# Second mixer: three blocks of the first token tile at its start, and two transposes queued later

## The chip, the cores and the metric

One core of one Trainium2 chip runs the whole program in one launch. The metric is device microseconds from launch to end; the number used is the median of several runs. Engines in the profile: PE is TensorE (PEld its weight loads), DVE is VectorE, ACT is ScalarE, POOL is GpSimd, SP is SyncE, which issues the transfers.

## The reference, cut to what matters

The program computes two blocks, each of two layers, on 256 tokens of width 1024, in float32. The first block has, per layer, a feed-forward part, a mixer and a second feed-forward part. The second block has, per layer, one mixer and one feed-forward part. The change touches only the mixer of the second block, so it acts twice in a run:

```python
h = rms_norm(x, norm_mix_g) * (1 + sc_m) + sh_m
proj = h @ w_in                                   # (256, 1024) @ (1024, 5024)
(qa, ka, va, cq, ckv, kr, qc, kc, vc, ga, gb, gc) = jnp.split(proj, idx, axis=-1)
o_na  = neighborhood_attention(qa, ka, va, na_rpb)            # 4 heads of 64
q_b   = rms_norm(cq, mla_q_norm_g) @ mla_w_uq                 # cq: 256 columns
kv_b  = rms_norm(ckv, mla_kv_norm_g) @ mla_w_ukv              # ckv: 128 columns
k_pe  = rope_2(kr, pos_t)                                     # kr: 32 columns
o_mla = blocked_attention(q_full, k_full, v_b, ...)           # 4 heads of 96
q_c   = axial_rope(rms_norm(qc), pos_row, pos_col)            # 8 heads of 64
k_c   = axial_rope(rms_norm(kc), pos_row, pos_col)            # 2 heads of 64
o_gqa = blocked_attention(q_c, k_c, v_c, ...)
merged = sigmoid(ga) * (o_na @ w_br_na) + sigmoid(gb) * (o_mla @ w_br_mla) + sigmoid(gc) * (o_gqa @ w_br_gqa)
x = x + g_m * (merged @ w_out)
```

## The kernel before

**Precision and weights.** Every big product is made of three matmuls on pairs (high part, rest), so each weight unit (128 rows by up to 1024 numbers) is loaded by a transfer, cast on ACT to its high part (`prep_H`, line 321) and subtracted on DVE for the rest (`prep_L`, through the helper of line 185). A block of 512 columns of `w_in` is four units, each of two row steps (kt); one unit of 832 columns belongs to the odd block of 416 columns.

**The planner's clock.** While the program is written out, `pump` advances a clock of its own: 0.648 for a row step of a 512-column block, 0.528 for one of the 416-column block, 0.327 for one of `gemmA`. On each pump one more unit is prepared if `hold` is off, fewer than `WH` units are live, and 1.2 have gone by since the last one. `hold` is set when the last results of a stage are merged, and `fin_b` for the second tile clears it. Work given to `later` or `spawn` is written out when that clock reaches its due time. Afterwards a list scheduler orders each engine's instructions by its own estimate of what is ready; on the chip each engine works through its list in that order.

**Tokens.** There are two token tiles of 128. The input of the mixer for tile 1 is finished late: `fin_a` makes the normalised tile (line 198), and `pend()`, which is `fin_b` for tile 1, transposes it on PE (line 182), scales it on DVE and ACT (lines 200 and 206) and splits it into `uH` (line 214) and `uL`.

**The opening of the mixer (`mix2`).** Block b0 holds the 512 columns of qc, block b1 va and cq, block b2 (the odd one, 416 columns) ckv, kr, kc and vc, and one more block holds qa and ka. The order of PE's work is: b0 for tile 0, half of b1 for tile 0, `pend()`, the other half, b0 for tile 1, b1 for tile 1, then `gemmA` for qa and ka (both tiles at once, in two halves). Then two lanes of neighbourhood attention start, and beside them come b2 for tile 0 and tile 1, then the gates. The products go to two PSUM banks of tag A in turn, so a block can start only when the copy of the block before the last has left its bank: line 1454 for q of tile 0, line 1464 for q of tile 1, line 1442 for b1, line 1493 for b2.

**After a block.** `q_post` squares q on ACT, sums on DVE (line 1408), takes the root on POOL (lines 219 and 221), and 3.45 of the planner's clock later multiplies, rotates (`rope`, line 185) and, another 5.6 later, transposes the heads on PE (four transposes from `m` to `T`) and copies them out (line 1426). The same chain runs for the keys in b2. `low_rank` normalises cq or ckv and transposes it 4.5 later (`gain_T`).

**Buffers.** SBUF tiles of 4 KB per partition share one pool of 36 (`m4`, tag s4): units, loads on their way, and the copies of q1, of b1 and of b2 among them. Tiles of 2 KB share a pool of 15 (`m2`). At the start of the mixer eight units are prepared, those of b0 and b1; `WH` is 8.

Of the kernel before, what the change touches and what calls it, by code (L numbers as in the profile page):

```python
# [103 lines left out]
class K:  # L104
# [1254 lines left out]
    def mix2_plan(self, l):  # L1359
        a = self.a  # L1360
        w = a["w_in_2_blk"][l]
        for i in (2, 1, 0):
            self.plan_cols(w[i])
        self.plan_cols(a["w_in_2_odd"][l])
        gate = lambda i: self.plan_cols(w[3 + i])
        gate(0)
        self.unit(2, a["mla_w_uq_2"][l])
        self.unit(1, a["mla_w_ukv_2"][l])
        gate(1), gate(4)
        self.plan_rows(a["w_br_na_2"][l], 0, 2)  # L1370
        gate(5), gate(2)
        self.plan_rows(a["w_br_gqa_2"][l], 0, 4)
        gate(3)
        self.plan_rows(a["w_br_mla_2"][l], 0, 2)
        self.plan_rows(a["w_out_2"][l], 0, 8)

    def mix2(self, l, u, pend):
# [24 lines left out]

        def gqa_norm(ps, nh, tab, tt, fin, pair=False):
            n = nh * 64
# [6 lines left out]
            def rest():  # L1411
                qn = self.m2([128, 512])
                self.mul(v(qn[:, :n], nh), v(ps, nh), r[:, :nh].unsqueeze(2).to_broadcast([128, nh, 64]))
                o = self.m2([128, 512])
                self.rope(o, qn, nh, 64, tab[:, 0, tt], tab[:, 1, tt], 2, pair)
                yield 5.6
                fin(o)
# [3 lines left out]
        def q_post(tt, ps):  # L1421
# [5 lines left out]

            gqa_norm(ps[:, :], 8, gt[0], tt, fin, True)

        def low_rank(ps, n, H, L, g):  # L1430

            sq = self.m2([128, 512])
            ss = self.sm([128, 1])
            self.act(sq[:, :n], ps, AF.Square, accum_out=ss)
            r = self.rstd(ss, 1, n)
            c = self.m2([128, 256])
            self.ts(c[:, :n], ps, r, ALU.mult)
            self.later(4.5, lambda: self.gain_T(c, H, L, g, n // 128))

# [9 lines left out]

        b0, b1 = self.blk(), self.blk()  # L1450
        p = self.pA()
# [3 lines left out]
        p = self.pA()  # L1455
        self.gemmB(u, b1, 0, p, k1=4)
        pend()
        q_post(0, q0)
        self.gemmB(u, b1, 0, p, k0=4)
        vc_post(0, p)  # L1460
        p = self.pA()
        self.gemmB(u, b0, 1, p, last=True)
# [4 lines left out]
        self.gemmB(u, b1, 1, p, last=True)  # L1467
        vc_post(1, p)

        qaT, kaT = self.m2([128, 2, 256]), self.m2([128, 2, 256])  # L1470
# [13 lines left out]
        lanes = [self.spawn(na[0:1], 0.95), self.spawn(na[1:2], 3.5)]  # L1484

        kvH, kvL = self.m2([128, 2, 128], F32R), self.m2([128, 2, 128], F32R)
        kpe = self.t([128, 2, 32], "kpe", 1)
        b = self.blk()
        for tt in range(2):
            p = self.pA()  # L1490
            self.gemmB(u, b, tt, p, 416, last=tt == 1)
            kv = self.m4([128, 512])
            nc.scalar.copy(kv[:, :416], p[:, :416])
            p = kv
            low_rank(p[:, 0:128], 128, kvH[:, tt:tt + 1], kvL[:, tt:tt + 1], self.vec("mkn", l, 1))
            self.rope(kpe[:, tt], p[:, 128:160], 1, 32, self.cs("mlac", tt * 32, 32), self.cs("mlas", tt * 32, 32), 1)
            nc.scalar.copy(vd[:, tt], p[:, 288:416])

            def fin(o, tt=tt):
                q = self.pT()  # L1500
                self.tr(q[:, 0:128], o[:, 0:128])
                nc.scalar.copy(kgT[:, tt * 128:tt * 128 + 128], q[:, 0:128])

            gqa_norm(p[:, 160:288], 2, gt[1], tt, fin)

# [382 lines left out]
```

## Time and profile before

| | |
|---|---|
| median of 3 runs | 1924.72 us (1924.52 to 1927.49) |
| the profiled execution, its own time | 1923.49 us |
| its span, first to last instruction | 1921.7 us |
| PE, PEld, DVE, ACT, POOL busy | 98%, 81%, 76%, 51%, 3% |
| granted TensorE clock, mean | 0.996 |
| opening of the second mixer, layer 0 | about 1134 to 1190 us of the span |
| opening of the second mixer, layer 1 | about 1526 to 1580 us of the span |

The busy share of PE says how little is left in all. What a change in one stage is worth is read from that stage: the stretches in which PE stands still, what it waited for, and how long its matmuls take just afterwards. All times below are microseconds from the start of the span. In a timeline row the bracket at the end gives how long the engine was idle before the row, and which instruction ended that idle time.

### The profile page before, as it was taken

The page shows a single profiled execution, that of the slowest core. Times are in us where ns is not written, and L with a number is a line of the kernel's source. Part 1 is how long each engine was busy: PE and PEld are TensorE (multiplying, and loading weights), DVE is VectorE, ACT ScalarE, POOL GpSimd, SP SyncE. Part 2 cuts the span into 40 slices and gives each one's busy share as a digit, 9 for nine tenths or more (in the row PEclk, how much of TensorE's full clock was granted, in tenths as well). Part 3 has the DMA queues.
Part 4 walks back from the last instruction along what each step waited for, and adds up shares of the span by engine and source line. Part 5 has one row for each costly group of instructions (what it writes and reads, how often), then busy time and mean ns, then how long its engine had stood idle before and what let it go on. Part 6 is the DMA issues. An engine that isn't in the chain of part 4 may idle for free.

```text
span 1921.7 us, 25594 instructions
## 1 busy us (share of the span) xinstructions
PE 1884.8 (98%) x9240; PEld 1554.0 (81%) x9240; DVE 1455.0 (76%) x2254; ACT 988.6 (51%) x1649; POOL 66.5 (3%) x135
## 2 busy tenths in 40 slices
PE   8999999999999999999999989999999999999998
PEld 6888798888888888988888878777888887778886
DVE  8877788787878877696878767678878776787552
ACT  6544566554445444476644445744544457546441
POOL 0000000100000000000100021000000110000000
PEclk9999999999999999999999999999999999999999
DMA  9997685488877987764498856468888763676540
GB/s 393 343 339 282 227 299 197 134 293 311 314 262 275 315 322 250 267 215 143 174 322 307 299 152 178 141 235 291 297 313 313 203 184 123 217 273 228 192 161 22
DMA packets 139056, 471.17 MB, mean 245 GB/s; under 512 B 24273, under 2 KB 24497, under 8 KB 138802
## 3 DMA queue, kind: packets, MB, share of 16 engines
q1 hardware_dynamic: 138930, 469.55, 70.3%
q8 instruction: 72, 1.18, 0.2%
q14 instruction: 54, 0.44, 0.1%
HBM read 468.40 MB, written 1.10 MB: 244 GB/s over the span
## 4 chain that ended last, share of the span: by engine, by line
PE 65%; issue 27%; DVE 4%; ACT 1%; POOL 1%; DMA 1%; SPq 0%; DVEq 0%; POOLq 0%; ACTq 0%
PE A L170 42%; PE B L170 19%; PE T L182 3%; DVE s L185 2%; DVE m L185 1%; DMA s<-in_ada_w 1%; PE T L170 1%; ACT m L206 0%; ACT s L321 0%; DVE s L515 0%; POOL sm L229 0%; POOL sm L221 0%; DVE h L185 0%; DVE m L203 0%; DVE s L203 0%
## 5 line engine op out<-in xcount | busy, mean ns | idle before, releaser
L170 PE MATMUL A<-s,uH 128*128 128x512 f32 (+1 forms) x2976 | 933.3, 394 | 2.1 <-ACT uH L214 1.4
L185 DVE TENSOR_TENSOR s<-s,s 128x1024 fp32r<-128x1024 f32 (+2 forms) x638 | 753.4, 1198 | 110.1 <-ACT s L321 104.0
L321 ACT CAST s<-s 128x1024 fp32r<-128x1024 f32 (+1 forms) x618 | 621.9, 1043 | 47.9 <-DVE s L185 28.7
L170 PEld LDWEIGHTS A<-s,uH 128*128 128x128 f32 x2976 | 548.0, 188 | 119.2 <-issue 7.3
L170 PE MATMUL A<-s,uL 128*128 128x512 f32 (+1 forms) x1488 | 579.9, 391 | 1.5 <-DVE uL L185 1.5
L170 PE MATMUL B<-s,m 128*128 128x512 f32 (+2 forms) x1696 | 407.4, 387 | 1.2 <-ACT m L214 1.1
L170 PEld LDWEIGHTS B<-s,m 128*128 128x128 f32 x1696 | 309.7, 189 | 62.8 <-ACT m L214 2.9
L170 PEld LDWEIGHTS A<-s,uL 128*128 128x128 f32 x1488 | 279.5, 188 | 61.1 <-DVE uL L185 4.0
L515 DVE SCALAR_TENSOR_TENSOR s<-s,cb 128x1024 f32<-128x1024 f32 x256 | 310.6, 1217 | 4.0 <-DMA s<-in_ada_w 3.4
L206 ACT ACTIVATE m<-A 128x256 f32<-128x256 f32 x126 | 48.3, 383 | 287.1 <-PE A L170 286.9
L214 ACT CAST m<-T 128x256 fp32r<-128x256 f32 x132 | 48.8, 372 | 205.7 <-PE T L182 205.7
L185 DVE TENSOR_TENSOR m<-m,A 128x256 f32<-128x256 f32 x126 | 52.6, 418 | 112.4 <-ACT m L206 111.8
L170 PE MATMUL A<-uH,s 128*128 128x256 f32 (+1 forms) x672 | 129.6, 289 | 2.7 <-ACT s L1442 2.3
L170 PEld LDWEIGHTS A<-uH,s 128*128 128x128 f32 (+1 forms) x672 | 107.0, 191 | 4.5 <-ACT s L1442 2.8
L170 PE MATMUL B<-s,s 128*128 128x512 f32 (+3 forms) x432 | 103.1, 383 | 2.5 <-DVE s L203 2.0
L170 PE MATMUL A<-uL,s 128*128 128x256 f32 (+1 forms) x336 | 96.3, 286 | 0.0
L185 DVE TENSOR_TENSOR m<-T,m 128x256 fp32r<-128x256 f32 x132 | 55.1, 420 | 54.2 <-ACT m L214 54.0
L170 PEld LDWEIGHTS B<-s,s 128*128 128x128 f32 (+1 forms) x432 | 78.6, 188 | 18.3 <-DVE s L203 2.9
L182 PE MATMUL T<-ident,m 128*128 128x128 f32 (+1 forms) x488 | 84.3, 273 | 8.1 <-DVE m L185 6.6
L182 PEld LDWEIGHTS T<-ident,m 128*128 128x128 f32 (+1 forms) x488 | 62.9, 139 | 35.2 <-DVE m L185 9.1
L206 ACT ACTIVATE m<-h 128x512 f32<-128x512 f32 x44 | 27.8, 632 | 84.3 <-DVE h L185 84.3
L170 PEld LDWEIGHTS A<-uL,s 128*128 128x128 f32 (+1 forms) x336 | 64.1, 191 | 0.7
(190 smaller groups left out, 1197.9 us busy)
## 6 DMA issues: line engine op xcount, KB each, us to landing
s<-in_ffn_gu SPq DMA_DIRECT2D x264, 512.0 KB, 5.2
s<-in_ada_w SPq DMA_DIRECT2D x240, 512.0 KB, 5.8
s<-in_w_in_blk SPq DMA_DIRECT2D x152, 512.0 KB, 4.8
s<-in_ffn_wd SPq DMA_DIRECT2D x88, 512.0 KB, 5.5
s<-in_ffn_w_down SPq DMA_DIRECT2D x44, 512.0 KB, 4.7
s<-in_w_out SPq DMA_DIRECT2D x40, 512.0 KB, 4.2
s<-in_final_ada_w SPq DMA_DIRECT2D x16, 512.0 KB, 6.5
s<-row SPq DMA_DIRECT2D x12, 512.0 KB, 6.5
```

The source lines that it names most:

```text
L170: self.last = self.nc.tensor.matmul(out, l, r, start=start, stop=stop, skip_group_check=True)
L182: self.nc.tensor.transpose(out, in_, self.ident[:p, :p])
L185: self.nc.vector.tensor_tensor(o, x, y, op=op)
L206: return self.nc.scalar.activation(o, x, f, **kw)
L214: self.nc.scalar.copy(H, x)
L321: self.last_H = self.nc.scalar.copy(H[:, :n], raw[:, :n])
L515: self.nc.vector.scalar_tensor_tensor(raw, raw, 1.0, self.cb, op0=ALU.mult, op1=ALU.mult, accum_out=v)
```

## The change

It moves b2 from after `gemmA` to the opening: b2 for tile 0 follows b1 for tile 0, b2 for tile 1 follows b1 for tile 1. The units of the odd block are therefore planned before those of qa and ka. `WH` is 12 during the opening and 8 after it. `hold` is cleared after the first half of b1, and `pend()` and `q_post` for tile 0 come after the whole of b1. The head transposes of q are due 9.0 instead of 5.6 after the rotation, those of the keys 7.0 instead of 5.6, and the transposes of `low_rank` 6.5 instead of 4.5.

```diff
 def mix2_plan(self, l):
-        for i in (2, 1, 0):
+        for i in (2, 1):
             self.plan_cols(w[i])
         self.plan_cols(a["w_in_2_odd"][l])
+        self.plan_cols(w[0])
...
-        def gqa_norm(ps, nh, tab, tt, fin, pair=False):
+        def gqa_norm(ps, nh, tab, tt, fin, wait, pair=False):
...
-                yield 5.6
+                yield wait
                 fin(o)
...
-            gqa_norm(ps[:, :], 8, gt[0], tt, fin, True)
+            gqa_norm(ps[:, :], 8, gt[0], tt, fin, 9.0, True)
...
-            self.later(4.5, lambda: self.gain_T(c, H, L, g, n // 128))
+            self.later(6.5, lambda: self.gain_T(c, H, L, g, n // 128))
...
-        b0, b1 = self.blk(), self.blk()
+        kvH, kvL = self.m2([128, 2, 128], F32R), self.m2([128, 2, 128], F32R)
+        kpe = self.t([128, 2, 32], "kpe", 1)
+
+        def odd_post(tt, p):
+            kv = self.m4([128, 512])
+            nc.scalar.copy(kv[:, :416], p[:, :416])
+            low_rank(kv[:, 0:128], 128, kvH[:, tt:tt + 1], kvL[:, tt:tt + 1], self.vec("mkn", l, 1))
+            self.rope(kpe[:, tt], kv[:, 128:160], 1, 32, self.cs("mlac", tt * 32, 32), self.cs("mlas", tt * 32, 32), 1)
+            nc.scalar.copy(vd[:, tt], kv[:, 288:416])
+
+            def fin(o):
+                q = self.pT()
+                self.tr(q[:, 0:128], o[:, 0:128])
+                nc.scalar.copy(kgT[:, tt * 128:tt * 128 + 128], q[:, 0:128])
+
+            gqa_norm(kv[:, 160:288], 2, gt[1], tt, fin, 7.0)
+
+        self.WH = 12
+        b0, b1, b2 = self.blk(), self.blk(), self.blk()
         p = self.pA()
         self.gemmB(u, b0, 0, p)
         q0 = self.m2([128, 512])
         nc.scalar.copy(q0, p)
         p = self.pA()
         self.gemmB(u, b1, 0, p, k1=4)
+        self.hold = False
+        self.gemmB(u, b1, 0, p, k0=4)
         pend()
         q_post(0, q0)
-        self.gemmB(u, b1, 0, p, k0=4)
         vc_post(0, p)
+        p = self.pA()
+        self.gemmB(u, b2, 0, p, 416)
+        odd_post(0, p)
         p = self.pA()
         self.gemmB(u, b0, 1, p, last=True)
...
         self.gemmB(u, b1, 1, p, last=True)
         vc_post(1, p)
+        p = self.pA()
+        self.gemmB(u, b2, 1, p, 416, last=True)
+        odd_post(1, p)
+        self.WH = 8
...
         lanes = [self.spawn(na[0:1], 0.95), self.spawn(na[1:2], 3.5)]
-
-        kvH, kvL = self.m2([128, 2, 128], F32R), self.m2([128, 2, 128], F32R)
-        kpe = self.t([128, 2, 32], "kpe", 1)
-        b = self.blk()
-        for tt in range(2):
-            p = self.pA()
-            self.gemmB(u, b, tt, p, 416, last=tt == 1)
...
```

The lines removed at the end did for b2 what `odd_post` now does.

## Rows read from the trace of the kernel before

**Rows 1.** The page's first part: busy time, share of the span and instructions of each engine.

```profile
PE 1884.8 (98%) x9240; PEld 1554.0 (81%) x9240; DVE 1455.0 (76%) x2254; ACT 988.6 (51%) x1649; POOL 66.5 (3%) x135
```

**Rows 2.** Stretches: window, length, busy PE, PEld, DVE, ACT, POOL; clock, DMA, GB/s.

```profile
1145.00:1150.00 5.00, 2.27 (x13) 1.61 (x13) 3.90 (x9) 2.19 (x6) 1.51 (x4) 1.00 0.60 156
...
1170.00:1175.00 5.00, 3.84 (x21) 3.60 (x20) 3.03 (x5) 4.15 (x8) 1.05 (x2) 0.66 0.64 168
```

**Rows 3.** Timeline of PE, opening of layer 0: start, length, instruction, [idle before].

```profile
1146.29 1.09 PE L182 MATMUL T<-ident,s 128*128 128x128 f32 x8 [1.39 <-DVE s L198]
...
1149.52 0.73 PE L170 MATMUL A<-s,uH 128*128 128x512 f32 x2 [1.45 <-ACT uH L214]
...
1150.58 0.62 PE L170 MATMUL A<-s,uH 128*128 128x512 f32 x2
...
1157.93 0.66 PE L182 MATMUL T<-ident,m 128*128 128x128 f32 x4 [0.57 <-DVE m L185]
...
1169.60 0.66 PE L182 MATMUL T<-ident,m 128*128 128x128 f32 x4 [1.40 <-DVE m L185]
1171.42 0.58 PE L170 MATMUL A<-uH,s 128*128 128x256 f32 x1 [1.16 <-ACT s L1442]
...
1174.58 0.41 PE L170 MATMUL A<-uH,s 128*128 128x256 f32 x2
...
1174.94 0.40 PE L170 MATMUL A<-uH,s 128*128 128x256 f32 x2
```

**Rows 4.** Timeline of PE, opening of layer 1.

```profile
1534.87 1.03 PE L182 MATMUL T<-ident,s 128*128 128x128 f32 x8
...
1546.76 0.66 PE L182 MATMUL T<-ident,m 128*128 128x128 f32 x4 [0.79 <-DVE m L185]
...
1551.15 0.28 PE L170 MATMUL A<-uH,s 128*128 128x256 f32 x1
...
1558.43 0.66 PE L182 MATMUL T<-ident,m 128*128 128x128 f32 x4 [1.36 <-DVE m L185]
1560.24 0.57 PE L170 MATMUL A<-uH,s 128*128 128x256 f32 x1 [1.16 <-ACT s L1442]
...
1563.89 0.40 PE L170 MATMUL A<-uH,s 128*128 128x256 f32 x2
```

**Rows 5.** Timeline of DVE, opening of layer 0.

```profile
1145.74 0.88 DVE L198 TENSOR_SCALAR s<-h,sm 128x512 f32<-128x512 f32 x2 [2.69 <-POOL sm L229]
...
1150.86 0.69 DVE L185 TENSOR_TENSOR uL<-m,uH 128x512 fp32r<-128x512 f32 x1 [0.67 <-ACT uH L214]
```

**Rows 6.** The chain of waits, layer 1: start, length, what.

```profile
1548.36 2.68 DVE s L185 x3
```

**Rows 7.** Timeline of ACT, opening of layer 1.

```profile
1545.16 0.59 ACT L1464 COPY s<-A 128x512 f32<-128x512 f32 x1
...
1559.12 0.58 ACT L1426 COPY s<-T 128x512 f32<-128x512 f32 x1 [8.72 <-PE T L182]
1559.60 0.59 ACT L1442 COPY s<-A 128x512 f32<-128x512 f32 x1
```

**Rows 8.** Groups by form, 1500 to 1600: xcount, busy us, mean ns.

```profile
L185 DVE TENSOR_TENSOR s<-s,s 128x832 fp32r<-128x832 f32 x4 | 4.1, 1018 | 0.0
```

**Rows 9.** Timeline of PE, layer 0: b2, the last attention output, the branches.

```profile
1182.42 0.53 PE L170 MATMUL A<-s,uH 128*128 128x416 f32 x2
...
1182.98 0.54 PE L170 MATMUL A<-s,uH 128*128 128x416 f32 x2
...
1282.28 1.08 PE L170 MATMUL B<-m,m 128*64 128x256 f32 x8
...
1284.09 11.05 PE L170 MATMUL A<-s,s 128*128 128x512 f32 x48
...
1300.42 2.88 PE L170 MATMUL A<-s,m 128*128 128x512 f32 x12
```

**Rows 10.** Waits of the transfer queue, 1120 to 1200: total us, times, longest.

```profile
SPq L306 <- PE A L170: 28.1, 11, 8.7
```

More of the change, by code (lines that the diff above doesn't have):

```diff
@@ L1484, in mix2 @@
         lanes = [self.spawn(na[0:1], 0.95), self.spawn(na[1:2], 3.5)]
-        kvH, kvL = self.m2([128, 2, 128], F32R), self.m2([128, 2, 128], F32R)
-        kpe = self.t([128, 2, 32], "kpe", 1)
-        b = self.blk()
-        for tt in range(2):
-            p = self.pA()
-            self.gemmB(u, b, tt, p, 416, last=tt == 1)
[L1492 to L1504, printed above, removed]
         gq = []
```

## The prediction

> **What bounds the kernel now.** The page's first part comes first: PE is busy 98% of the span [rows 1], so a change of order can win only what PE loses by standing still or by running slow. Next, the table by stretches over both openings of the second mixer: the reader is to see PE busy for 2.27 of 5 us in one stretch, and in another 3.84 of 5 at a granted clock of 0.66 [rows 2]. Then the timeline of PE, for what ended each pause.
>
> Layer 0 has five pauses in the opening [rows 3]. 1.39 us before the transposes of tile 1's input, which wait for the normalised tile. 1.45 us for `uH`, made from those transposes, because only one row step of b1 was left to run meanwhile. 0.57 and 1.40 us before the head transposes of q for tile 0 and tile 1, which wait for the end of the rotation on DVE. 1.16 us before the second half of `gemmA`, whose bank is still held: the copy of b1's tile 1 (line 1442) stands on ACT right behind the copy of those transposes. Sum 5.97.
>
> Layer 1 [rows 4] has its input transposes without a pause, then 0.79, 1.36 and the same 1.16. Sum 3.31.
>
> After the long pauses PE runs slow. From 1171.42 to 1174.58 five steps of `gemmA` take 3.16 us; the step from 1174.58 to 1174.94 takes 0.36, so 1.36 us are lost [rows 3], in a stretch that was partly at the 1.2 GHz level. In layer 1 six steps from 1560.24 to 1563.89 take 3.65 instead of 2.16: 1.49 lost [rows 4]. The step from 1149.52 to 1150.58 takes 1.06 us [rows 3], against 3 × 0.23 = 0.69 (48 matmuls of 512 columns in 11.05) [rows 9]: 0.37 lost. All that the change can reach: 5.97 + 3.31 + 1.36 + 1.49 + 0.37 = 12.5 us, 0.65% of the time.
>
> **The change part by part.** No matmul is added or removed, so PE's own work stays.
>
> *b2 of tile 0 after b1.* It is 8 steps of 0.56 [rows 9], 4.5 us of PE work. Because `pend()` now follows the whole of b1, the input transposes start one step (0.69) later in PE's list; the tile that they wait for is as late as before, so in layer 0 of the 1.39 some 0.7 remain. Behind them b2 covers the 1.45 of `uH`: from the transposes at 1146.29 to the end of `uL` at 1150.86 + 0.69 it is 5.3 us, of which the transposes take 1.1, and b2 4.5 of the rest. Both goes with its slow step: 0.7 + 1.45 + 0.37 = 2.5 us won. In layer 1 nothing was lost there, and nothing is won.
>
> *Its weights.* b2 now needs four odd units that were prepared long after. Each costs DVE 1.02 us [rows 8], 4.1 in all, and ACT a little less. `hold` is cleared half a block earlier for them. In layer 0 DVE stands idle for 2.69 us before the normalised tile [rows 5], which takes two; the other two have to fit in smaller gaps or they run behind `uL`. Their loads take the places in SP's queue that qa and ka's had, so they are issued earlier than before. I take 0; the bounds are 0 and what the third rival gives.
>
> *Head transposes later.* For tile 0 the emission moves from 9.05 to 12.45 of the planner's clock after the q post-processing, behind b2, b0 of tile 1 and half of b1: at least 3.4 us more of work ahead of it, against pauses of 0.57 and 0.79. These go (1.36). For tile 1: 12.45 is 8 × 0.648 + 8 × 0.528 + 9.3 × 0.327. On the chip that is 24 matmuls of 0.23 (5.5), b2 (4.5), 9.3 steps of 0.36 (3.35) and about 0.7 of other transposes: 14.1 us after b0. The chain before took from the copy at 1545.16 to 1558.43, 13.3 us [rows 4, 7]; in it DVE did three weight subtractions in a row (2.68) ahead of the sum [rows 6]. So 0.8 is to spare, and against it stand the key work of b2's tile 0 on the same DVE and the units that `WH` 12 admits. I take 0.6 of waiting left per layer; bounds 0 and the old 1.4. Won: 1.40 + 1.36 - 1.2 = 1.6.
>
> *The bank of `gemmA`'s second half.* Line 1442 for tile 1 is now followed by b2, so it has a block more. In its place stands the copy of b2's tile 1. If the head transposes come at step 9 of `gemmA` and the half is at step 16, there are 6.7 × 0.36 = 2.4 us between them, enough for two copies of 0.59 [rows 7]. I take half of the old pause left: 2 × 0.6. Won 2.32 - 1.2 = 1.1. With no pause of the old size before it, the slow steps go as well: 2.85.
>
> *Attention.* The lanes start one b2 (both tiles, 9 us) later against the rest. What is late next would be the branches: the last attention output ran at 1282.28 and its branch at 1300.42 [rows 9], 17 us after its end, so 8 remain. Within the lanes the work gets denser beside the gates, but DVE is rid of b2's key work there; neither is priced by a row, so the bounds are a gain and a loss of 1.4 per layer, the size of the largest pauses of [rows 3], and I take a loss of 0.5 in all.
>
> Sum: 2.5 + 1.36 + 1.6 + 1.1 + 2.85 - 0.5 = 8.9 us. The profiled execution took 1923.49, of which the span is 1921.7; so 1914.6, and 1.2 more for the median of the runs: 1915.8.
>
> **The rivals.**
>
> *The bubble is a lack of buffers.* Line 1442 ran at 1559.60, 8.45 us after PE had turned from b1 to `gemmA` at 1551.15, with ACT idle for 8.72 [rows 4, 7]; it stands behind the head copy, though it was written out first, and besides that block it wants only a free s4 tile. Transfers waited 28.1 us, 11 times, for PE to free tiles [rows 10]. If the pool of 36 holds it up, the copy of b2's tile 1 at the same place, with 12 units (24 tiles) live, is held up alike, whatever is queued later. Then 1.40 + 1.16 + 1.36 and 1.36 + 1.16 + 1.49 stay, 7.9 of the 12.5, with the 0.7: 12.5 - 7.9 - 0.7 - 0.5 = 3.4 won, 1921.3. Against it: on ACT it follows the head copy at once, and that one is late through the transposes. The Trainium skill (Perfetto Trace Analysis, Identifying Performance Opportunities) says that the same gap repeating on the engine that should be saturated can mean that there is no room for the next tile; by that rule the pause of 1.16 stays in both layers. The trace agrees on the repetition: 1.16 twice.
>
> *The scheduler keeps its order.* It places the transposes by its own estimate, so a later due time might not move them; then only the 2.5 of layer 0 is won, less 0.5: 1922.7. For it: before, the transposes of tile 1 stood 16 steps into `gemmA` ((1558.43 - 1.36 - 1551.15) / 0.36 [rows 4]), though their due time is 3.87 / 0.327 = 12 steps in. Against it: that is a move to later; the pauses come of places too early, and a later due time only adds.
>
> *Weights late.* If the four subtractions run behind `uL`, the last ends at 1151.55 + 4.1 = 1155.6, while PE wants that unit 6 steps into b2, at 1147.4 + 3.4 = 1150.8: 4.8 us, and some 1.4 of slow steps, in layer 0. Won 8.9 - 6.2 = 2.7: 1922.0. Against it: the idle 2.69.
>
> *Slower: evictions starve.* Five copies of each opening need an s4 tile, and 24 are units, at least 4 loads, 2 biases, and the copies before. If three copies are as late as line 1442 was (8.45), PE, with one other block as cover, waits 8.45 - 5.5 = 2.95 for b1 of tile 1, the same for b2 of tile 1, and 8.45 - 4.5 = 3.95 for `gemmA`, with 1.4 of slow steps: 11.2 per layer, 22.5 in all against 12.5 won: 1934.7. It decides the sign from 6.3 us per layer. Against it: the copies of b0 and of b1's tile 0 came at once; line 1442 alone was late, where for three quarters of `gemmA` no unit is given back, whereas the new copies but one stand in blocks that give back units.
>
> **How the numbers follow.** Chances: forecast 0.55 (own range 1911 to 1919.5), lack of buffers 0.17, weights late 0.12, order kept 0.06, starving 0.10. 0.2% is 3.85 us, about what a measurement can tell from no change: faster is below 1920.9, slower above 1928.6. Faster: 0.53 + 0.07 + 0.04 + 0.01 = 0.65. Slower: starving in most of its forms, 0.10. Same 0.25. The range goes from 1910.5 (all of the 12.5 and a little of the lanes) to 1924.5: outside are starving, 0.10, and tails of the others, some 0.1.
>
> **What would show it.** In layer 0, transposes from `s` with at most about 0.7 before them, then matmuls of 416 columns without a pause for `uH`. Head transposes of tile 1 inside the first half of `gemmA` with under 1 us before them; no stretch at 0.66 there. Wrong if PE waits for DVE's subtraction or ACT's cast of an odd unit within b2; if line 1493 or 1442 comes several us after its block and a block waits for it; or if the branches wait for attention.

## The result, and the profile after

The kernel after takes 1940.54 us (median of 4 runs, 1939.04 to 1941.89) against 1924.62 for the kernel before (4 runs, 1922.21 to 1927.49): ratio 1.0084, 95% interval 1.0072 to 1.0096. It is slower by 16 us, where 8.9 us faster was forecast; the time lies outside the range, and it is past the rival that was to end on the slower side.

The page's first part of the kernel after, which answers to [rows 1]:

```profile
PE 1888.6 (97%) x9240; PEld 1554.2 (80%) x9240; DVE 1456.4 (75%) x2254; ACT 989.1 (51%) x1649; POOL 70.7 (4%) x135
```

The work is the same, instruction for instruction; PE takes 3.8 us more for it and stands still longer. To find where, each of the two mixers is cut into the opening (from b0 to the first up-projection of q) and the rest (from there to the last transposes ahead of the output product). The table of stretches of the kernel before, opening and rest of layer 0, opening and rest of layer 1 (window, length, busy PE, PEld, DVE, ACT, POOL, granted clock, DMA share, GB/s):

```profile
1134.53:1203.19 68.66, 62.00 (x332) 52.44 (x331) 52.78 (x109) 39.23 (x85) 16.68 (x32) 0.98 0.60 162
1203.19:1321.54 118.35, 116.11 (x582) 89.33 (x581) 91.46 (x158) 66.29 (x130) 2.94 (x4) 1.00 0.62 216
1526.55:1592.14 65.59, 61.58 (x331) 52.90 (x332) 48.94 (x105) 39.17 (x83) 11.97 (x20) 0.97 0.64 170
1592.14:1709.05 116.91, 116.06 (x583) 89.32 (x581) 88.24 (x149) 66.27 (x130) 2.94 (x4) 1.00 0.59 202
```

The same four of the kernel after:

```profile
1132.48:1204.53 72.05, 63.06 (x329) 53.02 (x328) 52.50 (x107) 38.35 (x81) 18.87 (x32) 0.95 0.58 160
1204.53:1327.39 122.86, 117.26 (x586) 89.51 (x585) 92.61 (x162) 68.25 (x137) 2.58 (x4) 1.00 0.59 208
1532.42:1601.27 68.85, 62.32 (x329) 52.55 (x329) 48.50 (x102) 37.07 (x77) 15.24 (x21) 0.95 0.59 161
1601.27:1725.02 123.75, 119.49 (x586) 90.88 (x584) 89.46 (x152) 69.00 (x137) 2.58 (x4) 0.99 0.54 192
```

The lengths differ by 3.39, 4.51, 3.26 and 6.84: 18.0 us. The mixer of layer 0 starts 2.05 earlier in this execution, so the span grows by 16.0 (1921.7 to 1937.7). Of the 18.0, idle time of PE is 11.6 (length less busy, after less before) and slower matmuls 6.4. Only the smaller part, 6.65, is in the openings, about which nearly all of the forecast was; 11.35 is in the rest, for which it had 0.5.

**The opening.** The timeline of PE in layer 0 (start, length, instruction, idle before it and what ended it), to be read against [rows 3]:

```profile
1144.71 1.09 PE L182 MATMUL T<-ident,s 128*128 128x128 f32 x8 [1.19 <-DVE s L198]
...
1147.93 0.46 PE L170 MATMUL A<-s,uH 128*128 128x416 f32 x1 [0.50 <-DVE s L185]
...
1150.05 0.50 PE L170 MATMUL A<-s,uL 128*128 128x512 f32 x1 [0.45 <-DVE uL L185]
...
1155.28 0.46 PE L170 MATMUL A<-s,uH 128*128 128x416 f32 x1 [1.23 <-DVE s L185]
...
1164.36 0.66 PE L182 MATMUL T<-ident,m 128*128 128x128 f32 x4 [0.52 <-DVE m L203]
...
1171.34 0.28 PE L170 MATMUL A<-uH,s 128*128 128x256 f32 x1
...
1178.75 0.66 PE L182 MATMUL T<-ident,m 128*128 128x128 f32 x2 [4.74 <-DVE m L198]
...
1181.13 1.06 PE L182 MATMUL T<-ident,m 128*128 128x128 f32 x4
```

The reader is to see three things. The pause of 1.45 for `uH` and the 1.16 ahead of `gemmA`'s second half are gone. b2 waits for subtractions of odd units (0.50 and 1.23), and its eight steps do not run in one piece: after four of them the list has PE begin b0 of tile 1, at 1148.99, where it waits 0.45 for `uL`. And 2.67 us into `gemmA` (1171.34 to 1174.01) there is one new pause of 4.74, ahead of two transposes: these are the low-rank transposes of tile 1 (the two of cq), which waited for nothing in the kernel before:

```profile
1175.42 0.38 PE L182 MATMUL T<-ident,m 128*128 128x128 f32 x2
```

The four head transposes of tile 1 follow at 1181.13 without a pause, because all had been standing still already. Layer 1, against [rows 4]:

```profile
1552.11 0.45 PE L170 MATMUL A<-s,uH 128*128 128x416 f32 x1 [0.40 <-DVE s L185]
...
1561.70 0.66 PE L182 MATMUL T<-ident,m 128*128 128x128 f32 x4
...
1567.10 0.33 PE L182 MATMUL T<-ident,m 128*128 128x128 f32 x1 [0.60 <-DVE m L203]
...
1576.09 0.66 PE L182 MATMUL T<-ident,m 128*128 128x128 f32 x2 [4.83 <-DVE m L198]
```

The four head transposes of tile 0 (1561.70) wait for nothing here, but the single one of b2's keys (1567.10) does. Behind both of the long pauses the steps of `gemmA` are slow again; the window from 1576 to 1580 was granted 0.50, all of it at 1.2 GHz:

```profile
1576.00:1580.00 4.00, 3.91 (x19) 3.94 (x20) 1.95 (x5) 1.46 (x4) 0.00 (x0) 0.50 0.89 320
```

What the low-rank transposes wait for is read from DVE's list in layer 0:

```profile
1173.71 1.22 DVE L185 TENSOR_TENSOR s<-s,s 128x1024 fp32r<-128x1024 f32 x1
1174.84 0.90 DVE L185 TENSOR_TENSOR m<-m,g 128x128 f32<-128x128 f32 x4
1175.65 1.22 DVE L185 TENSOR_TENSOR s<-s,s 128x1024 fp32r<-128x1024 f32 x1
1176.78 0.69 DVE L185 TENSOR_TENSOR m<-m,m 128x512 f32<-128x512 f32 x1
1177.38 0.95 DVE L185 TENSOR_TENSOR s<-s,s 128x768 fp32r<-128x768 f32 x1
1178.25 0.35 DVE L198 TENSOR_SCALAR m<-s,sm 128x256 f32<-128x256 f32 x1
```

The last row, 0.35 us, is what PE wants. Its scale was there when the root on POOL ended, at 1174.21. Then it stood for 4 us behind three subtractions of weights (`s<-s,s`: two of 1024 columns, one of 768) and q's rotation (`m<-m,...`). Further up the chain, ACT copied b1 out of its bank only at 1170.24, 3.5 us after b1's last matmul, behind casts of more weights, one of which had itself waited 1.13 us for its transfer, and POOL took q's root (2.52 us) ahead of this one. DVE does about as much as before in this stage (52.50 us against 52.78); it does it in another order.

**The rest.** Before, PE waited for nothing at the up-projections. After, in layer 0 (layer 1 has 1.73, 1.22 and 0.67 at the same places):

```profile
1207.92 3.06 PE L170 MATMUL A<-s,m 128*128 128x512 f32 x12 [1.73 <-ACT s L206]
1212.17 0.64 PE L182 MATMUL T<-ident,m 128*96 128x128 f32 x4 [1.19 <-POOL m L1564]
1213.49 0.32 PE L182 MATMUL T<-ident,m 128*96 128x128 f32 x1 [0.67 <-ACT s L1578]
```

ACT's list in the same stretch:

```profile
1202.17 0.51 ACT L206 ACTIVATE m<-m,sm 128x256 f32<-128x256 f32 x1
...
1205.59 0.50 ACT L206 ACTIVATE m<-m,sm 128x256 f32<-128x256 f32 x1
...
1206.08 1.03 ACT L321 CAST s<-s 128x1024 fp32r<-128x1024 f32 x1
1207.01 0.36 ACT L1560 COPY m<-A 128x256 f32<-128x256 f32 x1
1207.28 0.59 ACT L206 ACTIVATE s<-A 128x512 f32<-128x512 f32 x1
```

The row at 1207.28 is the tanh of gate 0's second tile, which empties the bank that the second product of the up-projections needs; PE had written it by about 1204.7. It stands behind exponentials of attention (256 columns each; the rows left out between 1202.17 and 1205.59 are more of them, their sums and a cast). In the kernel before, the exponentials ahead of it were over at 1201.7, the up-projections began at 1203.19, and the tanh came 1.5 us later:

```profile
1204.71 0.60 ACT L206 ACTIVATE s<-A 128x512 f32<-128x512 f32 x1
```

In layer 1 of the kernel after, the steps behind these pauses ran slow as well: the windows from 1608 and from 1612 (4 us each) were granted 0.84 and 0.73.

### The profile page after: what moved, and what is told of

It is laid out like the page before. It is cut to its first block, busy times and chain, and to the rows that moved or that the text cites. A ratio compares the mean times of both kernels' runs of the same rounds, so it can differ in the third digit from the quotient of the medians.

```text
span 1937.7 us, 25609 instructions
## 1 busy us (share of the span) xinstructions
PE 1888.6 (97%) x9240; PEld 1554.2 (80%) x9240; DVE 1456.4 (75%) x2254; ACT 989.1 (51%) x1649; POOL 70.7 (4%) x135
## 4 chain that ended last, share of the span: by engine, by line
PE 64%; issue 27%; DVE 4%; DMA 2%; POOL 1%; ACT 1%; SPq 0%; DVEq 0%; POOLq 0%; ACTq 0%
PE A L170 41%; PE B L170 19%; PE T L182 3%; DVE s L185 1%; DMA m<-in_na_rpb 1%; DMA s<-in_ada_w 1%; DVE m L185 1%; ACT m L206 1%; PE T L170 1%; POOL sm L221 0%; ACT s L321 0%; SPq L1690 0%; DVE s L515 0%; POOL sm L229 0%; DVE h L185 0%
## 5 line engine op out<-in xcount | busy, mean ns | idle before, releaser
L185 DVE TENSOR_TENSOR s<-s,s 128x1024 fp32r<-128x1024 f32 (+1 forms) x638 | 753.6, 1199 | 119.3 <-ACT s L321 113.1
L321 ACT CAST s<-s 128x1024 fp32r<-128x1024 f32 (+2 forms) x618 | 622.4, 1042 | 43.9 <-DVE s L185 28.7
L182 PEld LDWEIGHTS T<-ident,m 128*128 128x128 f32 (+1 forms) x488 | 63.4, 140 | 46.1 <-issue 11.7
```

The costliest lines, as they stand in the source:

```text
L182: self.nc.tensor.transpose(out, in_, self.ident[:p, :p])
L185: self.nc.vector.tensor_tensor(o, x, y, op=op)
L321: self.last_H = self.nc.scalar.copy(H[:, :n], raw[:, :n])
```

## The experiments

Two theories came out of this reading, one for each place:

- Theory 1, the opening: b2 pulls the low-rank transposes of tile 1 forward in PE's time, and the units that `WH` 12 lets in, with q's own chain, stand ahead of their normalisation on ACT, POOL and DVE.
- Theory 2, the rest: because b2 is no longer beside attention, the lanes run one b2 later against the gates, and the up-projections now meet their exponentials on ACT.

Each rival is named in the expectations. The edits are against the kernel after, or against the kernel before where the label begins with it. All times and ratios:

| run | us, median (runs) | ratio to before, 95% interval |
|---|---|---|
| after | 1940.54 (4) | 1.0084 (1.0072 to 1.0096) |
| lowrank_later | 1935.73 (5) | 1.0063 (1.0049 to 1.0077) |
| ahead_8 | 1939.57 (5) | 1.0081 (1.0069 to 1.0094) |
| order_only | 1944.49 (4) | 1.0105 (1.0091 to 1.0118) |
| ahead_12_b2_only | 1936.56 (5) | 1.0063 (1.0051 to 1.0075) |
| gate1_ahead | 1931.87 (5) | 1.0039 (1.0026 to 1.0052) |
| before_lanes_late | 1934.91 (5) | 1.0059 (1.0046 to 1.0071) |
| ahead_12_b2_gate1 | 1926.19 (12) | 1.0007 (0.9999 to 1.0016) |
| due_times_new_order | 1928.63 (6) | 1.0029 (1.0018 to 1.0041) |
| all_later | 1920.08 (11) | 0.9980 (0.9971 to 0.9989) |
| all_later_still | 1920.81 (11) | 0.9986 (0.9977 to 0.9995) |
| before_heads_later | 1925.00 (11) | 1.0004 (0.9995 to 1.0012) |
| before_both_later | 1919.39 (11) | 0.9978 (0.9969 to 0.9987) |
| before_second_later | 1918.76 (11) | 0.9977 (0.9968 to 0.9986) |

The kernel before took 1923.18 to 1924.62 us beside these runs, from one group of them to the next, so a difference between two rows is good to some 1.5 us.

### The opening

**lowrank_later.**

```diff
-            low_rank(ps[:, 256:512], 256, cqH[:, tt], cqL[:, tt], self.vec("mqn", l * 2, 2))
+            low_rank(ps[:, 256:512], 256, cqH[:, tt], cqL[:, tt], self.vec("mqn", l * 2, 2), (6.5, 11.0)[tt])
```

> The kernel after (1940.5 us), with one number changed: the low-rank transposes of q's second token tile are due 11.0 instead of 6.5 after their normalisation. Theory 1 (PE meets these transposes some 7 us after b1's second tile, while their chain stands on ACT, DVE and POOL behind the preparation of later weights and behind q's own chain): the pause of 4.74 us in layer 0 and of 4.83 in layer 1 goes, and with the one in layer 1 about 1.4 us of slow steps; 9 to 11 us won, 1930 to 1932. Theory 2 (what costs is that the up-projections now meet the lanes' exponentials, 1.73 + 1.2 + 0.67 us of pauses per layer and slow steps behind them): that stage stays as long as in the kernel after (122.9 and 123.8 us against 118.4 and 116.9 before) and the time stays over 1929. Rival (DVE is simply full there, so whatever PE asks for next is late): the pause moves to the next transposes or to the second half of gemmA, and the time stays at 1938 to 1941.

Measured: 1935.73, 4.8 us won, about half of what theory 1 gave. PE in layer 0 and in layer 1:

```profile
1177.49 1.09 PE L182 MATMUL T<-ident,m 128*128 128x128 f32 x4 [2.52 <-DVE m L185]
...
1571.67 0.65 PE L182 MATMUL T<-ident,m 128*128 128x128 f32 x4 [2.48 <-DVE m L185]
```

With the two low-rank transposes out of the way, the four head transposes of tile 1 are the next to be late, and they wait for the end of the rotation, as the rival said: 2.5 of the 4.8 us stay. So both chains of tile 1 were late, not one, and the low-rank pause had only stood in front. In layer 1 a third one shows: the single low-rank transpose of ckv, from b2's tile 1, waits 1.84 us (1577.76).

**ahead_8.** The line `self.WH = 12` ahead of the blocks, and `self.WH = 8` behind them, are left out.

> The kernel after without the change of the units prepared ahead (8 throughout, not 12 in the opening). Theory 1: the casts and subtractions of gate 0 and of the q up-projection no longer stand ahead of the low-rank chain, so that the pause of 4.7 us falls to 2.5 or less per layer: 3 to 5 us won there, and no more than 2 lost where gate 0's units are prepared later; 1935 to 1939. Rival 1 (q's own chain, the rotation and the root on POOL, makes that chain late, not the units): the pause stays at 4 to 5 us, and the time at 1939 to 1942. Rival 2 (b2's odd units are then late): new pauses of 1 to 5 us for DVE's subtraction within b2, 1942 to 1950.

Measured: 1939.57, no real gain. Both answers are in the trace at once. Layer 0:

```profile
1152.46 0.45 PE L182 MATMUL T<-ident,m 128*128 128x128 f32 x1 [5.77 <-ACT s L321]
...
1178.90 0.44 PE L182 MATMUL T<-ident,m 128*128 128x128 f32 x2 [1.21 <-DVE m L198]
```

The low-rank pause falls from 4.74 to 1.21 (layer 1: 4.83 to 1.11), as theory 1 has it: the units prepared ahead made that chain late. But then b2 of tile 0 waits 5.77 us for a cast in layer 0 (its matmuls follow the row shown at 1152.56), as rival 2 has it. In layer 1 it waits 0.58 and 0.92 us for odd units, between these b0 of tile 1 waits 1.63 for `uH`, and `gemmA` 1.22 for a unit of its own. The 12 units are needed up to b2 and harmful behind it.

**ahead_12_b2_only** separates the two.

```diff
         self.gemmB(u, b2, 0, p, 416)
+        self.WH = 8
         odd_post(0, p)
...
         odd_post(1, p)
-        self.WH = 8
```

> The kernel after, but the limit of units prepared ahead goes back from 12 to 8 as soon as b2 of the first token tile is through (the kernel after keeps 12 until b2 of the second tile). Theory 1: the odd units still come in time, and the units of gate 0 and of the q up-projection are no longer ahead of the low-rank chain of the second tile; the pause of 4.7 us falls to about 1.2 as with 8 throughout, without that run's 5.8 us for an odd unit: 5 to 8 us won, 1932 to 1936. Rival 1 (what is then late are units of b0, b1 or gate 0): new pauses of 1 to 4 us for a cast or a subtraction (lines 321 and 185) in the blocks behind, 1937 to 1942. Rival 2 (q's own chain makes the low-rank chain late): the pause stays over 4 us, 1939 to 1942.

Measured: 1936.56, 4.0 us won, 0.6 above the expected band. The pause is 1.62 in layer 0 and 1.71 in layer 1, without the 5.77:

```profile
1177.37 0.63 PE L182 MATMUL T<-ident,m 128*128 128x128 f32 x2 [1.62 <-DVE m L198]
```

Some of rival 1 comes with it: 0.43 us in layer 0 and 0.37 and 0.57 in layer 1 for subtractions of `gemmA`'s own units. In layer 0 two single transposes from b2's tile 1, of ckv and of the keys, now wait 0.60 and 0.73.

**order_only.** The due times of the kernel before (5.6 for the heads, 4.5 for the low-rank ones) in the new order.

> The kernel after with the old due times (5.6 for the head transposes, 4.5 for the low-rank ones), so the new order of blocks alone. Theory 1: the head transposes of tile 0 and 1 wait again as before the change (0.6 to 1.4 us each), and the low-rank transposes of tile 1 are met still earlier, so their pause is 5 us or more: 1941 to 1948. Rival (the later due times are what cost, since everything behind the transposes comes later): the time falls to 1925 to 1935.

Measured: 1944.49, 4 us worse, so the later due times were not what cost. Against what was expected, the largest pauses are not the low-rank ones but those of the head transposes of tile 1, 4.88 in layer 0 and 3.35 in layer 1:

```profile
1180.24 1.08 PE L182 MATMUL T<-ident,m 128*128 128x128 f32 x4 [4.88 <-DVE m L185]
```

### The rest of the mixer

**gate1_ahead.**

```diff
-        gate(0)
+        gate(0), gate(1)
         self.unit(2, a["mla_w_uq_2"][l])
...
-        gate(1), gate(4)
+        gate(4)
...
+        gate(1)
         qmT = self.m4([128, 4, 256])
...
-        gate(1)
+        gate(4)
         if not last.done:
...
-        gate(4)
```

> The kernel after, with the second gate (and its units in the loading plan) put ahead of the up-projections instead of behind them, so that these run one gate later against the lanes. Theory 2: the pauses in the up-projections (1.73, 1.19 and 0.67 us in layer 0; 1.73, 1.22 and 0.67 in layer 1) and the slow steps behind them in layer 1 go, because the lanes' exponentials are then behind; 7 to 11 us won, 1930 to 1933, with both openings as long as in the kernel after (72 and 69 us). Rival (the copy of a gate stands behind exponentials on ACT wherever it is, so that only the place of the pause changes): the second gate gets the pause, and the time stays at 1938 to 1942.

Measured: 1931.87, 8.7 us won. The openings keep their pauses (5.01 and 4.04 us at the low-rank transposes), and at the up-projections PE no longer waits (layer 0, first tile; the second, at 1224.54, does not either):

```profile
1221.67 1.93 PE L170 MATMUL A<-s,m 128*128 128x384 f32 x9
```

Neither gate took the pause over; the largest wait left in that stretch is 0.28. The rival falls.

**before_lanes_late** makes the loss without the change.

```diff
-        lanes = [self.spawn(na[0:1], 0.95), self.spawn(na[1:2], 3.5)]
+        lanes = [self.spawn(na[0:1], 9.4), self.spawn(na[1:2], 11.95)]
```

> The kernel before, with both attention lanes started one b2 (8.45 of the planner's clock for its two tiles) later and nothing else changed, so the openings stay as they were. Theory 2 (the up-projections lose when the lanes' exponentials come as late as in the kernel after): the stage from the up-projections on gets the pauses of about 1.7, 1.2 and 0.7 us per layer and the slow steps behind them, 7 to 11 us slower than before, 1931 to 1935. Rival 1 (the block order is needed for it, since b2's own work on ACT and DVE now stands elsewhere): within 2 us of before, 1922 to 1926. Rival 2 (late attention is late at its end, too): a wait of the branches for attention's last outputs, over 1936.

Measured: 1934.91, 11.7 us slower than the kernel before beside it (1923.18), in the old order of blocks. In layer 0 (layer 1 has the same 3.35, at 1600.07):

```profile
1207.32 4.52 PE L170 MATMUL A<-s,m 128*128 128x512 f32 x12 [3.35 <-ACT s L206]
```

One pause of 3.35 instead of three of 3.6 in all, and slow steps behind it (0.64 and 0.58 of the clock in the 4 us windows around them). The branches wait for nothing. Cut at the same places, the rest of the mixer takes 124.1 and 123.8 us (118.35 and 116.91 before, 122.86 and 123.75 after). So the lateness of attention is enough by itself, and the place where it costs is the bank that ACT empties too late, not attention's end.

### Do the two add up, and is anything left of the gain?

**ahead_12_b2_gate1**: the edits of ahead_12_b2_only and gate1_ahead together.

> The two edits together on the kernel after: the limit of 12 only until b2 of the first tile is through, and the second gate ahead of the up-projections. If the opening and the up-projections lose on their own, the gains add: 8.7 us (gate) and 5 to 8 us (limit), 1924 to 1927, no better than the kernel before. Rival (the opening's late units only push the loss into the gates): 1929 to 1933.

Measured: 1926.19, 14.4 us below the kernel after; the single gains were 4.0 and 8.7. They add, within the error, and the time is that of the kernel before.

**due_times_new_order**: ahead_12_b2_only, with the low-rank transposes of tile 1 due 11.0 and its head transposes due 12.0 instead of 9.0; gates as after.

> The kernel after with the openings mended (limit of 12 only until b2 of the first tile, low-rank transposes of the second tile due 11.0, its head transposes 12.0) and the gates where they are in the kernel after. If opening and up-projections lose on their own, this run is 7 to 11 us slower than the run all_later, which has the second gate ahead as well: 1927 to 1931, with pauses of 1.73, 1.2 and 0.67 us at the up-projections. Rival (with the opening mended the lanes start earlier, too, and the up-projections no longer meet their exponentials): 1920 to 1924.

Measured: 1928.63, 11.9 us below the kernel after. The pauses of 1.73 (1.96 in layer 1) and 0.67 at the up-projections are still there, the one of 1.2 is not. The rival falls.

**all_later**: due_times_new_order and gate1_ahead together.

> The kernel after with the second gate ahead of the up-projections, the limit of 12 only until b2 of the first tile, the low-rank transposes of the second tile due 11.0 and the head transposes of the second tile due 12.0 (9.0 in the kernel after): PE asks for nothing of the second tile before the end of gemmA. If both places explain the whole loss, nothing of it is left and the gain of 3 to 9 us that the prediction hoped for appears: 1916 to 1922, at or below the kernel before. Rival (the block order keeps DVE full in the opening, and the pause moves to the evictions, the scores or the up-projections, which need these transposes): 1926 to 1931.

Measured: 1920.08, ratio 0.9980 (0.9971 to 0.9989): both places mended, it is 20.5 us below the kernel after and some 4 below the one before. In `gemmA` neither the four head transposes of tile 1 nor the two low-rank ones of cq (1181.74) wait any more. What waits 1.03 is a single transpose, that of ckv from b2's tile 1, as the width of 128 in the row of DVE ahead of it shows (cq has 256):

```profile
1178.99 0.60 PE L182 MATMUL T<-ident,m 128*128 128x128 f32 x4
...
1181.10 0.33 PE L182 MATMUL T<-ident,m 128*128 128x128 f32 x1 [1.03 <-DVE m L198]
...
1181.74 0.38 PE L182 MATMUL T<-ident,m 128*128 128x128 f32 x2
```

The row of DVE:

```profile
1180.77 0.28 DVE L198 TENSOR_SCALAR m<-s,sm 128x128 f32<-128x128 f32 x1
```

**all_later_still**: 14.0 for 12.0 and 13.5 for 11.0.

> The run all_later with the head transposes of the second tile due 14.0 instead of 12.0 and its low-rank transposes 13.5 instead of 11.0. Where these transposes still wait for DVE in all_later (1.03 and 0.46 us in layer 0, 0.58 and 0.80 in layer 1) they no longer do: 2 to 3 us faster, 1917 to 1918.5. Rival (the scores and the evictions then wait in their place, or nothing in these pauses is on the path): 1919.5 to 1922.

Measured: 1920.81, the same within the error. The expectation had read the pauses of all_later wrongly: those of 1.03 and 0.46 (0.58 and 0.80 in layer 1) are those of ckv and of the keys of b2's tile 1, whose due times this run does not touch. That of ckv is there as before (1.02, and 0.76 in layer 1); the keys' is gone in layer 0, where the two of cq wait 0.72 instead, and 0.51 in layer 1. So the time is that of the rival, but the run moved transposes that had not waited, and what the pauses of ckv and the keys cost stays untested.

### The due times in the old order

**before_heads_later.**

```diff
-                yield 5.6
+                yield wait
                 fin(o)
...
-            gqa_norm(ps[:, :], 8, gt[0], tt, fin, True)
+            gqa_norm(ps[:, :], 8, gt[0], tt, fin, 9.0, True)
```

> The kernel before, with q's head transposes alone due 9.0 instead of 5.6 (b2 stays behind the attention's start, low-rank transposes stay at 4.5). If the prediction's step 'head transposes later' was sound in itself and only the new order of blocks spoiled it: the pauses of 0.57, 1.40 and 1.16 us in layer 0 and 0.79, 1.36 and 1.16 in layer 1 go, and the slow steps (1.36 and 1.49): 5 to 9 us won, 1915 to 1920. Rival (the transposes that come next, the low-rank ones or gemmA's second half, wait in their place for the same DVE work): 1922 to 1926.

Measured: 1925.00, ratio 1.0004 (0.9995 to 1.0012): nothing won. All the pauses named are gone, and in both layers one stands in their place:

```profile
1173.69 0.44 PE L182 MATMUL T<-ident,m 128*128 128x128 f32 x2 [3.73 <-DVE m L198]
...
1562.83 0.44 PE L182 MATMUL T<-ident,m 128*128 128x128 f32 x2 [3.94 <-DVE m L198]
```

Together with the heads' old pause the low-rank transposes had been just in time; PE now comes to them that much sooner, and the heads of tile 1 come behind them (1175.86). The rival holds, and it is the step that the forecast lacked.

**before_both_later**: the same, and the low-rank transposes of tile 1 due 11.0 instead of 4.5.

> The kernel before, with q's head transposes due 9.0 instead of 5.6 (as in the run before_heads_later) and the low-rank transposes of q's second tile due 11.0 instead of 4.5; block order and attention as before. Theory 1: in before_heads_later the low-rank transposes took over the wait (3.73 and 3.94 us) because they stayed where they were; with both later nothing of the second tile is asked for in gemmA's first half, and the pauses of 0.57, 1.40, 1.16 us (layer 0) and 0.79, 1.36, 1.16 (layer 1) go with their slow steps: 5 to 9 us faster than before, 1915 to 1919, at or below the best run with the new order (1920.1). Rival 1 (the wait moves on once more, to the scores of attention, which follow gemmA directly in this order and come from the same engines): 1922 to 1926. Rival 2 (the new order of blocks brings the gain of the best run, not the due times): 1922 to 1926, with the pause of 1.45 us for the first tile's input still there.

Measured: 1919.39, ratio 0.9978 (0.9969 to 0.9987). No more than the due times, in the old order, does as well as the best of the new order. The time lies between theory 1's 1915 to 1919 and rival 1: the pause of the heads of tile 1 is still there, longer than in the kernel before (2.18 in layer 1):

```profile
1169.80 0.66 PE L182 MATMUL T<-ident,m 128*128 128x128 f32 x4 [1.96 <-DVE m L185]
```

**before_second_later**: the heads of tile 1 due 13.0, its low-rank transposes 13.0.

> The kernel before with the block order and the attention lanes as they were, and due times set so that PE asks for nothing of the second tile in the first part of gemmA: q's head transposes 9.0 (first tile) and 13.0 (second), the low-rank transposes of the second tile 13.0. If the due times alone carry the gain: the pauses of 1.96 us (layer 0) and 2.18 (layer 1) that before_both_later still had before the second tile's head transposes go, with 1 to 1.5 us of slow steps each; 4 to 7 us below that run (1919.4), 1912 to 1916, clearly better than any run with the new order (1920.1). Rival 1 (as all_later_still against all_later: what is put off is then waited for at the scores): 1918 to 1922. Rival 2 (these transposes now delay the first scores and the lanes, so that the up-projections lose as in before_lanes_late): 1923 to 1930.

Measured: 1918.76, not below before_both_later by more than the error, and no lower than 1918 as rival 1 had it, but not for its reason: the pauses did not move to the scores, they did not move at all (2.22 in layer 1).

```profile
1170.27 0.66 PE L182 MATMUL T<-ident,m 128*128 128x128 f32 x4 [1.99 <-DVE m L185]
```

PE meets the head transposes of tile 1 about 5.9 us after the start of `gemmA` with a due time of 5.6 (the kernel before: 1162.30 to 1168.20), of 9.0 with the low-rank ones out of the way (1161.84 to 1167.84) and of 13.0 (1162.30 to 1168.28). In these three the list scheduler puts them at the same place whatever their due time; in before_heads_later, also with 9.0, they came later, behind the low-rank ones. The low-rank transposes of layer 0 did move, from 1177.18 in before_both_later to 1182.12. So what the old order could win without that pause is not known, and whether the new order is worth anything in itself stays open: with the due times set, the two stand level (1920.08 and 1918.76 to 1919.39, intervals overlapping). The gate order of gate1_ahead, part of all_later, was not run on the kernel before; there PE is idle for 2.24 and 0.85 us in the rest of the mixer, so it could win little. What is settled is that the gain over the kernel before does not need the new order.

## Why the prediction was wrong, step by step

The working is above; here each term with what it measured.

- **b2 after b1, 2.5 won in layer 0.** The 1.45 for `uH` went, and 1.19 instead of 0.7 stayed at the input transposes. But b2 waited 0.50 and 1.23 for odd units, and b0 of tile 1, begun after four of b2's eight steps, 0.45 for `uL`: 2.18 new against 1.65 gone, before the slow step. Nothing was won. Layer 1, costed at nothing, lost 0.40.
- **Its weights, 0.** The rival's 4.8 did not come, but not because two subtractions fitted into the 2.69. DVE still stands idle there:

```profile
1144.17 0.88 DVE L198 TENSOR_SCALAR s<-h,sm 128x512 f32<-128x512 f32 x2 [2.70 <-POOL sm L229]
```

Only the first two casts on ACT fell into that time; the subtractions ran behind the normalised tile, at 1144.97, 1146.86, 1154.20 and 1155.74. What that cost is 1.73 in layer 0 and 0.40 in layer 1. ahead_8 shows what the larger `WH` bought: without it 5.77.
- **Heads of tile 0, 1.36 won.** 0.84 won: 0.52 stayed in layer 0, nothing in layer 1. But four small pauses are new, of transposes that now come in the opening's first blocks: 0.33 in each layer for cq of tile 0 (line 198), and 0.36 and 0.60 in layer 1 for ckv and the keys of b2. On the other side 0.69 in each layer, at the transpose of ckv of tile 1 (1198.09 and 1587.03 in the kernel before), went, which the prediction had not listed.
- **Heads of tile 1, 0.6 left per layer.** In the kernel after no pause is seen there, but only because another stands in front. lowrank_later uncovers it: 2.52 and 2.48. In that run PE came no sooner than reckoned, 15.2 and 16.0 us after b0 of tile 1 against 14.1, and from the copy to the end of the rotation the chain took 14.0 and 14.2, little more than the 13.3. What the step left out is the time from the end of b0 to that copy. In the kernel before it was 1.0 us; here it is 3.5 and 4.2, since the copy (line 1487) stands on ACT behind casts of weights:

```profile
1161.44 1.99 ACT L321 CAST s<-s 128x1024 fp32r<-128x1024 f32 x2
1163.33 0.59 ACT L1487 COPY s<-A 128x512 f32<-128x512 f32 x1
```

With `WH` back at 8 behind b2 of tile 0 (ahead_12_b2_only) it comes 0.2 us after b0.
- **The bank of `gemmA`'s second half, 1.1 won.** All 2.32 went, but in the kernel after this by itself proves little: the copy of b2's tile 1 comes there at 1179.96, 8.6 us into `gemmA`, as late as line 1442 did (8.45), and the new pause stands in front. What tells against missing tiles is before_heads_later, the old order with the pool and the 8 units as they were and the heads' due times alone changed. There line 1442, behind the copy of tile 0's heads, comes 0.8 us into `gemmA` (1162.78), and the 1.16 is gone:

```profile
1163.54 0.59 ACT L1442 COPY s<-A 128x512 f32<-128x512 f32 x1
```

So the 1.16 was the copy of b1 behind the copy of the heads on ACT, and not, as far as SBUF goes, what the Trainium skill (Perfetto Trace Analysis, Identifying Performance Opportunities) gives as one possible cause of a repeating gap. Whether a third PSUM bank would have hidden it was not tested.
- **Slow steps, 2.85 won.** They came back behind the new pauses: in the openings PE's busy time grew by 1.06 and 0.74. The two stretches of the prediction hold 14 and 17 matmuls, a third of a step less than the five and six steps taken, so 0.12 more was lost in each.
- **The low-rank transposes: not priced at all.** This is the step that was missing in the opening. The change was read as making them later (4.5 to 6.5), and the prediction gave them no term. What counts is PE's work between their block and them. Before, 13.1 us went by (b1 ended at 1162.30, the transposes ran at 1175.42), of which 2.56 were the two pauses that were to go. After, b2 takes 8 × 0.528 = 4.2 of the 6.5, so they come 2.28 / 0.327 = 7 steps into `gemmA`, 7.3 us after b1 (about 1166.7 to 1174.01). Their chain took 11.9 us here (to 1178.6). It had not grown: in the kernel before it took 12.3, from 1162.30 to the end of this row of DVE:

```profile
1174.28 0.36 DVE L198 TENSOR_SCALAR m<-s,sm 128x256 f32<-128x256 f32 x1 [0.71 <-POOL sm L221]
```

So against the kernel before it is PE that came sooner; fewer units ahead of the chain (ahead_8, ahead_12_b2_only) shorten it, and pauses of 1.1 to 1.7 are left. The numbers needed stood in the code and in the timelines of before.
- **Attention, 0.5 lost, bounds 1.4 per layer.** This term failed worst: 4.51 and 6.84. The bounds were the largest pauses of the openings [rows 3], not a price of this stage, and the question "what is late next" was put to the branches alone, which indeed never waited. The row to look at was the tanh of gate 0 on ACT, and how many exponentials stand near it. gate1_ahead (8.7 won) and before_lanes_late (11.7 lost) show that this is the larger half.
- **The rival on the slower side** put the loss on copies that lack a buffer, 1934.7. Copies did come late: those of q, b1 and b2 of tile 1 start 3.6, 3.5 and 8.6 us after their blocks. But in each case ACT's list accounts for it: each follows at once on other rows, casts or the scaling of transposes that PE made late, and no row shows one waiting for a free tile. That the scheduler keeps its order was wrong for the new order; in the old one it was right for the heads of tile 1 in before_both_later and before_second_later, and wrong in before_heads_later.

The forecast's kind of error is one: it counted pauses to be taken away from PE and let the rest of PE's list stand where it was. before_heads_later shows it by itself: every pause that the step named was removed, and the time stayed.

## What to carry to other kernels

When a pause on the busiest engine is to go, list everything that the engine asks of the others in the next 10 us or so, and set the time of arrival of each against the end of its chain: the second-latest chain takes over, here 3.73 us for pauses of 0.57, 1.40 and 1.16. When a block moves, recount each delay behind it in the engine's own work, and for work that goes on beside it (here attention) find which short copy of the main path will stand behind its instructions in the same list. Try the due times alone before the order of the blocks: here they gave the whole gain.

## What the runs showed of the hardware that was not expected

The same pause does not always cost the same clock. In the last part of layer 0's mixer every one of these kernels has the same pause of 1.71 or 1.72 us ahead of the same 26 matmuls. In the kernel after they then took 6.19 us, in before 6.21; in gate1_ahead, ahead_8, ahead_12_b2_only, due_times_new_order and before_second_later 7.72 to 7.82:

```profile
1318.96 7.78 PE L170 MATMUL B<-s,s 128*128 128x512 f32 x26 [1.71 <-DVE s L203]
```

In gate1_ahead, from which this row is, the window from 1320 to 1324 was granted 0.65, so part of it ran at 1.2 GHz; PE had been idle for 1.71 and busy before. One execution of each kernel was profiled, so whether this goes with the kernel or with the execution is not known. A difference of 1.6 us between two profiled executions can be this alone, and so can part of what is called slow steps above; the medians of the runs, not the single executions, carry the verdicts.
